# One of four modulation vectors moved: from column blocks visited by TensorE in attention to whole rows summed by VectorE beside w_conv_out

## The chip, the core and the metric

The kernel runs on one core of a Trainium2 chip. A core has five engines that run on their own and meet through semaphores: TensorE (PE, with its weight loads PEld), VectorE (DVE), ScalarE (ACT), GpSimd (POOL) and SyncE (SP), whose queue issues nearly all of this kernel's DMAs, in order. The metric is the device time of one execution in microseconds. Every run computes one trunk layer for 128 context tokens and 512 latent tokens, 640 in all, with 1024 features.

## The reference

All weights are float32. `silu(c)` for the latent tokens and `silu(c_ctx)` for the context tokens each go through `w_ada` (1024 x 6144) and give six vectors of 1024: shift, scale and gate of the mixer, shift, scale and gate of the feed-forward part.

```
ada = silu(c) @ w_ada + b_ada          # one row for latent, one for context tokens
sh1, sc1, g1, sh2, sc2, g2 = split(ada, 6)
u = rms_norm(h, g_pre1) * (1 + sc1) + sh1
z = u @ w_in                           # q, k, v, B, C, x, gate_att, gate_conv
A  = attention(q, k, v) @ w_att_out
Bm = (B * dwconv3(C * x)) @ w_conv_out
h = h + g1 * rms_norm((sigmoid(ga) * A + sigmoid(gc) * Bm) @ w_o, g_post1)
u = rms_norm(h, g_pre2) * (1 + sc2) + sh2
h = h + g2 * rms_norm((silu(g) * val) @ w_down, g_post2)   # [g, val] = dwconv3(u @ w_up)
```

The change is about `g2`, the last sixth of `w_ada`'s columns. It is needed only at the very end, multiplied with `g_post2`, as one row per kind of token that is spread over all partitions.

## The kernel before

Each large product is done as three products of float32r parts: a weight tile is loaded as `raw`, ACT rounds it to `whi`, DVE subtracts to `wlo`, and TensorE does hi x hi, hi x lo and lo x hi (`mm3`, L182). The raw, hi and lo tiles come from rings of three buffers each. The order on TensorE, ACT and DVE is written out by hand: these engines work in program order. SP's order is made by a planner; its queue is strictly in order, and a DMA that waits holds back those behind it. Landings are counted on eight semaphores in turn.

The stages, with the start of each in the profiled execution: a prologue (0 to 62 us) with the first modulation and k, v; attention (62 to 264) for four key groups `g`, nine steps `i` each; w_att_out and a mixer stage of 19 pairs of columns of w_in (`mix`, L1252), to 564; w_conv_out in eight blocks of 128 columns (loop at L1416, 564 to 621); w_o in two halves, the first half in four quarters `q` (L1794); w_up, and w_down woven into it.

The remaining four vectors of the modulation, `g1`, `sc2`, `sh2` and `g2`, are computed in attention. A column block of 128 of w_ada is a DMA of 1024 x 128 elements (`ada_load`, L228), with rows of 512 bytes. `ada_mm` (L231) multiplies it: eight float32 products with 32 columns of `s32` as weights, in which the two vectors silu(c) and silu(c_ctx) stand in columns 30 and 31 of each 32; a slice of `s32` shifted by the row number puts the two results in their rows. The products go round over the four column strips of TensorE. Thirty-two blocks are done at places (g, i) of the steps, one or two at a time: `VISITS` (L682) says where, and a ring of loads (`ring`, L689) brings column blocks and the weight units of att_out through the same raw buffers. After each visit DVE adds the result into `acc` (`ada2_keep`, L252). At the end of attention `ada2_fold` (L260) sums over the strips, adds the bias, multiplies by the gains, and writes `mod`; `mod_rows` (L273) transposes all 64 rows and stores them to `bct` in DRAM, from which `bload` (L1464) later spreads a row over the partitions: `g1` into WR before w_o, `g2` into G2 near the end (L2034).

In the loop of w_conv_out, block j makes the split of block j + 1 (`vcut`, L1248), loads block j + 3 (`mload`, L1224), does two products over 320 tokens (`plain_gemm`, L1200), multiplies each by the gate (`times`), adds the attention branch, has ACT round the result and DVE subtract it (`minus`, L1155). Block 3's column block is loaded twice, at the end of the mixer and in this loop; the second load is the one used. The regions r0 and r1 hold UH and UL, the parts of u, until the last mix; from w_o's last quarter they hold parts of the next stage (ZB0, ZB1), and in between they are free.

Of the kernel before, what the change touches and what calls it, by code (L numbers as in the profile page):

```python
# [11 lines left out]
F32 = mybir.dt.float32  # L12
# [5 lines left out]
D = 1024  # L18
# [45 lines left out]
def trunk_layer(ctx, tc, x_prompt, x_sample, cache_k, cache_v, c, c_ctx, w_ada, b_ada, g_pre1, g_post1, g_pre2,  # L64
# [145 lines left out]
    feat = const.tile([128, 120], F32, name="feat")  # L210
    F_B, F_PRE1, F_POST1, F_PRE2, F_POST2, F_CONV = 16, 64, 72, 80, 88, 96
    scsh = const.tile([128, KT, 4], F32, name="scsh")
    mod = const.tile([128, 4, 2, KT], F32, name="mod")
    bct = dp.tile([64, 128], F32, name="bct")
    hd = dp.tile([NT, 128, D], F32, name="hd")
    actd = dp.tile([NJ, 128, NACT], F32, name="actd")
# [11 lines left out]
    def ada_load(raw, c0):  # L228
        nc.sync.dma_start(raw.rearrange("p (k c) -> p k c", c=128), w_ada[:, c0:c0 + 128].rearrange("(k p) c -> p k c", p=128))
# [10 lines left out]

    def ada2_load(i, room=None):
        ada_raw[i] = raw_tile() if room is None else room
        ada_load(ada_raw[i], (2, 4, 3, 5)[i // KT] * D + (i % KT) * 128)

    def ada2_mm(us, p=None):

# [13 lines left out]
    def ada2_fold(acc):  # L260
        p = ps1()
        for i in range(2):
            PE.matmul(p[:, 32 * i:32 * i + 32], acc[:, i * 128:(i + 1) * 128], sel, start=True, stop=True)
        for which in range(4):
            src = p[:, 16 * which:16 * which + 16].rearrange("p (f r) -> p r f", r=2)
            b = F_B + (2, 4, 3, 5)[which] * KT
            V.tensor_tensor(out=mod[:, which], in0=src, in1=feat[:, b:b + KT].unsqueeze(1).broadcast_to((128, 2, KT)), op=ALU.add)
            if which != 2:
                gn = (F_POST1, F_PRE2, None, F_POST2)[which]
                V.tensor_tensor(out=mod[:, which], in0=mod[:, which], in1=feat[:, gn:gn + KT].unsqueeze(1).broadcast_to((128, 2, KT)),  # L270
                                op=ALU.mult)

    def mod_rows(i0, n, pool, pt):  # L273

        m = n * 2 * KT
        PE.transpose(pt[0:m, 0:128], mod[:, i0:i0 + n].rearrange("p i r f -> p (i r f)"), ident)
        mrow = pool.tile([64, 128], F32, tag="mrow", name=nm("mrow"), bufs=1)
        V.tensor_copy(mrow[0:m, :], pt[0:m, 0:128])
        nc.sync.dma_start(bct[i0 * 2 * KT:i0 * 2 * KT + m, :], mrow[0:m, :])
# [312 lines left out]
    with tc.tile_pool(name="att", bufs=2) as at:  # L592
# [87 lines left out]


        VISITS = {}  # L682
        for at_, n in (((0, 4), 2), ((0, 6), 2), ((0, 8), 2), ((1, 1), 1), ((1, 4), 2), ((1, 6), 1), ((1, 8), 2), ((2, 1), 1), ((2, 4), 2),
                       ((2, 6), 1), ((2, 8), 2), ((3, 1), 2), ((3, 4), 2), ((3, 6), 2), ((3, 8), 2)):
            k = 6 + sum(len(x) for x in VISITS.values())
            VISITS[at_] = tuple(range(k, k + n))
        assert VISITS[3, 8][-1] == 4 * KT - 1
# [638 lines left out]
    for j in range(KT):  # L1326
        unit = next_unit()
        if j == 6:
            for n in range(3):
                mload(n)  # L1330
        if j < 6:
            for f in making[2 * j:2 * j + 2]:
                f()
        elif j == 7:
            adds = msums(0)
            adds[0]()
            mhi(0, 0)
            lo_of(("m", 0, 0))
            adds[1]()
            mhi(0, 1)  # L1340
            adds[2]()
            mload(3)
        outs = plain_gemm(j, *unit.parts, AH, AL)
        for out, (b0, b1) in zip(outs, BLKS):
            if j < 2:
                times(MA[:, j, b0:b1], out, MA[:, KT - 2 + j, b0:b1])
            else:
                S.activation(MA[:, j, b0:b1], out, AF.Copy)
        if j == 0:
            mod_rows(0, 4, sm_, bank(7))  # L1350


    BH = Halves(NTOK, F32R, "BH")
# [11 lines left out]
    def sigma(x, sign=1.0):  # L1365
        S.activation(x, x, AF.Sigmoid, scale=sign)
# [46 lines left out]
    mix_last(NP - 1)  # L1413
    sigma(ROWS[6])
    sigma(ROWS[7], -1.0)
    for j in range(KT):  # L1416
        if j + 1 < KT:
            vcut(j + 1)
        else:
            cut_upto(state["next"] + 1)  # L1420
        if j + 3 < KT:
            mload(2 * NP + j + 3)
        else:
            fetch(state["next"] + min(j - 4, 2))
        _, hi, lo = cut["v", j]
        outs = plain_gemm(j + 2, hi, lo, BH, BL)
        sg = ROWS[j]
        for out, (b0, b1) in zip(outs, BLKS):
            times(sg[:, b0:b1], out, sg[:, b0:b1])
        V.tensor_tensor(out=sg, in0=sg, in1=MA[:, j, :], op=ALU.add)  # L1430
        mh, ml = MH[j // 4][:, j % 4, :], ML[j // 4][:, j % 4, :]
        S.activation(mh, sg, AF.Copy)
        minus(ml, sg, mh.bitcast(F32))
# [9 lines left out]
    ZB0 = ra.tile([128, 4, 4, HALF], F32R, tag="r0", name="ZB0")  # L1443
    ZB1 = ra.tile([128, 4, 4, HALF], F32R, tag="r1", name="ZB1")
    ZB2, ZB3 = (ra.tile([128, 2, 4, HALF], F32R, tag=f"r2{x}", name=f"ZB{i}") for x, i in (("a", 2), ("b", 3)))
    for i, (z, a) in {"B11": (ZB0, 0), "B21": (ZB0, 2), "B22": (ZB1, 0), "T2": (ZB1, 2), "T1": (ZB2, 0), "T3": (ZB3, 0)}.items():
        TT[i] = (z[:, a], z[:, a + 1])
# [6 lines left out]
    def lent(name):  # L1454

        return tuple(x.rearrange("p k c -> p (k c)")[:, :1024] for x in TT[name])
# [337 lines left out]
    for q in range(4):  # L1794
        us.append(next_unit())
        if q == 0:
            half_load(3)
            taps_load()
            for t in range(3):
                row_load(t)  # L1800
            half_cut(3, lent("T3"))
        elif q == 1:
            half_load(0)
            half_cut(0)
        elif q == 2:
            half_load(1)
            plain_load(0, 0)
            plain_load(0, 1)
            ffn_taps(bank(7))
        else:  # L1810
            half_cut(1)
            half_load(2)
            for i, name in ((0, "T2"), (1, "T1")):
                hi_of((0, i), raws[0, i], lent(name))
                lo_of((0, i))
                plain_load(1, i)
        for t in range(NT):
# [315 lines left out]
```

## Time and profile before

| what | value |
|---|---|
| runs | 1118.63, 1118.83, 1120.03 us; median 1118.83 |
| the profiled execution | 1118.44 us, span 1116.3 us |
| TensorE's granted clock | 0.999 |
| moved by DMA | 129.60 MB, mean 116 GB/s |
| w_ada loads in attention | 512 KB each, median 4.0 us to landing |

The span is the time from the first to the last instruction of the program; 2.1 us of the execution lie around it. In the profile's rows a matmul's length includes the depth of its pipeline, so that of two neighbours the distance from start to start is the cost, not the length. "Idle before" is the time that an engine sat still before an instruction, with what released it.

### The profile page before, as it was taken

Reading aid. Unit: us, or ns where it says so; the run is one execution under the profiler, and the core shown is the slowest. Engines: PE = TensorE matmul, PEld = TensorE weight load, DVE = VectorE, ACT = ScalarE, POOL = GpSimd, SP = SyncE. Lnnn points to the kernel's source line nnn. Section 1 sums busy time; section 2 is a strip of 40 time slices with the busy share of each in tenths; the row PEclk is TensorE's granted clock in tenths of the full one; section 3 lists DMA queues with packets and bytes.
Section 4 is the critical chain, followed back from the end, with each engine's and each line's share of the span. In section 5 each row is a group of like instructions: output and inputs, shape, how many; then the busy total and the mean of one; then the engine's idle time right before and its main releaser. Section 6 shows DMA issues by size and latency. Waiting matters only on the chain.

```text
span 1116.3 us, 19771 instructions
## 1 busy us (share of the span) xinstructions
PE 1106.7 (99%) x7963; PEld 1021.7 (92%) x7963; DVE 795.9 (71%) x1305; ACT 577.3 (52%) x1020; POOL 146.8 (13%) x189
## 2 busy tenths in 40 slices
PE   8999999999999999999999999999999999999997
PEld 6788888888999999999999889999999999998886
DVE  5687766654647798889645457888888888889544
ACT  5576666665234454545522256654655455556432
POOL 1066566552000000000000012000000000000001
PEclk9999999999999999999999999999999999999999
DMA  9844223323222233223332644232333233315722
GB/s 325 240 126 141 85 72 105 104 77 115 77 77 76 77 95 95 76 78 97 92 113 74 212 151 155 72 112 90 117 107 101 91 108 107 118 62 179 261 95 95
DMA packets 177305, 129.60 MB, mean 116 GB/s; under 512 B 6274, under 2 KB 159422, under 8 KB 177214
## 3 DMA queue, kind: packets, MB, share of 16 engines
q1 hardware_dynamic: 177102, 128.30, 37.3%
q8 instruction: 63, 1.03, 0.4%
q14 instruction: 28, 0.23, 0.1%
q10 hardware_dynamic: 112, 0.04, 0.0%
HBM read 116.87 MB, written 11.45 MB: 115 GB/s over the span
## 4 chain that ended last, share of the span: by engine, by line
PE 97%; DMA 1%; DVE 1%; ACT 0%; SPq 0%; POOL 0%; issue 0%; DVEq 0%; ACTq 0%; POOLq 0%
PE b L1142 45%; PE b L185 9%; PE b L183 9%; PE b L184 9%; PE s L862 3%; PE s L183 3%; PE s L672 3%; PE s L886 3%; PE s L184 3%; PE s L185 3%; PE s L235 1%; PE s L383 1%; PE b L1679 1%; DMA araw<-in_w_ada_dram 1%; PE s L643 0%; PE b L1530 0%
## 5 line engine op out<-in xcount | busy, mean ns | idle before, releaser
L1142 PE MATMUL b<-ZB,whi 128*128 128x320 f32 x1024 | 226.1, 309 | 0.0
L1142 PEld LDWEIGHTS b<-ZB,whi 128*128 128x128 f32 x1024 | 171.9, 188 | 1.8
L1142 PE MATMUL b<-ZB,wlo 128*128 128x320 f32 x512 | 158.1, 309 | 0.0
L1142 PE MATMUL b<-MT,whi 128*128 128x320 f32 x608 | 134.3, 309 | 0.0
L1142 PEld LDWEIGHTS b<-MT,whi 128*128 128x128 f32 x608 | 101.6, 188 | 0.0
L1142 PEld LDWEIGHTS b<-ZB,wlo 128*128 128x128 f32 x512 | 96.2, 188 | 0.0
L1142 PE MATMUL b<-MT,wlo 128*128 128x320 f32 x304 | 94.1, 309 | 0.0
L849 POOL TENSOR_TENSOR pr<-pr,sm 128x640 f32<-128x640 f32 x64 | 80.0, 1260 | 58.2 <-DVE sm L848 55.8
L1129 ACT ACTIVATE whi<-SUM 128x1024 fp32r<-128x1024 f32 x40 | 42.2, 1055 | 77.3 <-DVE SUM L1594 74.8
L1624 DVE SCALAR_TENSOR_TENSOR Y<-C,cffn,Y 128x642 f32<-128x642 f32 x88 | 77.8, 884 | 0.9
L839 ACT ACTIVATE pr<-s,mx,rq 128x640 f32<-128x640 f32 x64 | 56.6, 885 | 34.7 <-DVE mx L826 31.2
L149 DVE TENSOR_TENSOR wlo<-raw,whi 128x1024 fp32r<-128x1024 f32 (+1 forms) x32 | 35.4, 1107 | 51.7 <-ACT whi L148 48.1
L1142 PE MATMUL b<-UL,whi 128*128 128x320 f32 x228 | 70.9, 311 | 0.0
L1142 PE MATMUL b<-UH,wlo 128*128 128x320 f32 x228 | 70.1, 307 | 0.0
L1142 PE MATMUL b<-UH,whi 128*128 128x320 f32 x228 | 69.4, 304 | 0.0
L1129 ACT ACTIVATE whi<-WB 128x1024 fp32r<-128x1024 f32 x38 | 40.1, 1055 | 55.7 <-DVE WB L1237 55.7
L1133 DVE TENSOR_TENSOR wlo<-raw,whi 128x1024 fp32r<-128x1024 f32 (+1 forms) x51 | 50.5, 1020 | 25.1 <-ACT whi L1129 24.3
L183 PE MATMUL s<-whi,UH 128*128 128x256 f32 (+1 forms) x197 | 64.0, 325 | 0.0
L821 DVE TENSOR_REDUCE mx<-s 128x1 f32<-128x640 f32 x64 | 52.5, 820 | 15.5 <-PE s L672 15.0
L1150 ACT ACTIVATE p<-b 128x320 f32<-128x320 f32 x78 | 34.1, 437 | 54.0 <-PE b L1142 52.1
L185 PE MATMUL s<-whi,UL 128*128 128x256 f32 (+1 forms) x197 | 59.9, 304 | 0.0
L184 PE MATMUL s<-wlo,UH 128*128 128x256 f32 (+1 forms) x197 | 59.8, 303 | 0.0
(354 smaller groups left out, 2945.7 us busy)
## 6 DMA issues: line engine op xcount, KB each, us to landing
raw<-in_w_in_dram SPq DMA_DIRECT2D x48, 512.0 KB, 3.7
RAW<-in_w_up_dram SPq DMA_DIRECT2D x40, 512.0 KB, 3.9
raw<-in_w_ada_dram SPq DMA_DIRECT2D x30, 512.0 KB, 4.0
raw<-in_w_down_dram SPq DMA_DIRECT2D x22, 512.0 KB, 5.6
actd<-Y SPq DMA_DIRECT2D x18, 321.0 KB, 2.5
XT<-in_w_ada_dram SPq DMA_DIRECT2D x9, 512.0 KB, 7.0
raw<-in_w_conv_out_dram SPq DMA_DIRECT2D x9, 512.0 KB, 3.6
raw<-in_w_att_out_dram SPq DMA_DIRECT2D x8, 512.0 KB, 3.6
```

Source lines behind the costliest of these rows:

```text
L149: V.tensor_tensor(out=lo[:, :n], in0=raw, in1=hi[:, :n].bitcast(F32), op=ALU.subtract)
L183: PE.matmul(out, ah, bh, start=start, stop=False)
L184: PE.matmul(out, ah, bl, start=False, stop=False)
L185: PE.matmul(out, al, bh, start=False, stop=stop)
L821: V.tensor_reduce(out=mx, in_=self.sc[h], axis=AX.X, op=ALU.max, negate=True)
L839: S.activation(pr, self.sc[h], AF.Exp, bias=mx, scale=rs, accum_out=sm)
L849: G.tensor_tensor(out=pr, in0=pr, in1=sm.broadcast_to((128, NTOK)), op=ALU.mult)
L1129: S.activation(to[0], raw, AF.Copy)
L1133: V.tensor_tensor(out=lo, in0=raw, in1=hi.bitcast(F32), op=ALU.subtract)
L1142: PE.matmul(out, p[:, ws], q[:, k, :], start=start and k == 0 and n == 0, stop=stop and k == 3 and n == 2, skip_group_check=True)
L1150: S.activation(t, pair[j][b], AF.Copy)
L1624: V.scalar_tensor_tensor(out=y, in0=crows(j)[i][:, d:d + NACT], scalar=cffn[:, 44 * d + o:44 * d + o + 1], in1=y, op0=ALU.mult, op1=ALU.add)
```

## The change

`mod` keeps three vectors; the eight column blocks of `g2` leave the ring and the visits, so that eight places of attention go from two blocks to one. `g2` is made in another way: eight loads of 128 whole rows of w_ada's last 1024 columns (4 KB a row) go into the free regions r0 and r1. For each load DVE multiplies the 128 x 1024 tile by silu(c), one number per partition, and adds it to a sum, and the same for silu(c_ctx): two operations per load, the first pair without the addition. They stand in blocks 1 to 7 of w_conv_out, one between the two `times` and one before ACT's rounding is used, and the last pair in w_o's first quarter. Four float32 products with `ones` (128 x 32) as weights then sum over the partitions, two halves of the columns times two rows, each on its own column strip; they stand in w_o's third quarter, behind the transposes of the convolution taps. DVE adds the bias, multiplies by sqrt(1024) and g_post2, which four DMAs have spread over 64 partitions each, and four stores of 2 KB put the result where `bload` reads it. The tiles of r0 and r1 for the next stage are declared later (`more_right`).

```
-    mod = const.tile([128, 4, 2, KT], F32, name="mod")
+    mod = const.tile([128, 3, 2, KT], F32, name="mod")
+    ones = const.tile([128, 32], F32, name="ones")
+    G.memset(ones, 1.0)
...
-        ada_load(ada_raw[i], (2, 4, 3, 5)[i // KT] * D + (i % KT) * 128)
+        ada_load(ada_raw[i], (2, 4, 3)[i // KT] * D + (i % KT) * 128)
...
-        for which in range(4):
+        for which in range(3):
...
-        for at_, n in (((0, 4), 2), ((0, 6), 2), ((0, 8), 2), ((1, 1), 1), ((1, 4), 2), ((1, 6), 1), ((1, 8), 2), ((2, 1), 1), ((2, 4), 2),
-                       ((2, 6), 1), ((2, 8), 2), ((3, 1), 2), ((3, 4), 2), ((3, 6), 2), ((3, 8), 2)):
+        for at_, n in (((0, 4), 2), ((0, 6), 2), ((0, 8), 2), ((1, 1), 1), ((1, 4), 1), ((1, 6), 1), ((1, 8), 1), ((2, 1), 1), ((2, 4), 1),
+                       ((2, 6), 1), ((2, 8), 1), ((3, 1), 1), ((3, 4), 1), ((3, 6), 1), ((3, 8), 1)):
...
-            mod_rows(0, 4, sm_, bank(7))
+            mod_rows(0, 3, sm_, bank(7))
...
+    GA0, GA1 = (region(ra, f"r{i}", [5, D], F32, f"GA{i}") for i in range(2))
+    gacc, gvec = GA0[:, 0:2, :], GA0[:, 4, :].rearrange("p (i c) -> p i c", i=2)
+    graws = [GA1[:, k, :] for k in range(5)] + [GA0[:, k, :] for k in (2, 3)] + [GA1[:, 0, :]]
+
+    def g2_load(k):
+        nc.sync.dma_start(graws[k], w_ada[k * 128:(k + 1) * 128, 5 * D:6 * D])
+
+    def g2_vectors():
+
+        for i, src in enumerate((b_ada[5 * D:6 * D].unsqueeze(0), g_post2)):
+            for h in range(2):
+                nc.sync.dma_start(gvec[64 * h:64 * h + 64, i, :], src[:, h * 512:h * 512 + 512].broadcast_to((64, 512)))
+
+    def g2_add(k, row):
+        x = s32[:, 32 * k + 30 + row:32 * k + 31 + row]
+        if k == 0:
+            V.tensor_scalar(out=gacc[:, row, :], in0=graws[k], scalar1=x, scalar2=None, op0=ALU.mult)
+        else:
+            V.scalar_tensor_tensor(out=gacc[:, row, :], in0=graws[k], scalar=x, in1=gacc[:, row, :], op0=ALU.mult, op1=ALU.add)
+
+    def g2_rows(p):
+
+        for h in range(2):
+            for row in range(2):
+                j = 64 * h + 32 * row
+                PE.matmul(p[j:j + 32, :], ones, gacc[:, row, h * 512:h * 512 + 512], start=True, stop=True, tile_position=(0, j),
+                          skip_group_check=True)
+        out = GA0[:, 3, 0:512]
+        V.tensor_tensor(out=out, in0=p, in1=gvec[:, 0, :], op=ALU.add)
+        V.scalar_tensor_tensor(out=out, in0=out, scalar=D ** 0.5, in1=gvec[:, 1, :], op0=ALU.mult, op1=ALU.mult)
+        for h in range(2):
+            for row in range(2):
+                j, r0 = 64 * h + 32 * row, (6 + row) * KT + 4 * h
+                nc.sync.dma_start(bct[r0:r0 + 4, :].rearrange("(o f) c -> o (f c)", o=1), out[j:j + 1, :])
+
     for j in range(KT):
+        if j == 0:
+            g2_load(0)
+        if j < KT - 1:
+            g2_load(j + 1)
+        if j == 5:
+            g2_vectors()
...
-        for out, (b0, b1) in zip(outs, BLKS):
+        for h, (out, (b0, b1)) in enumerate(zip(outs, BLKS)):
             times(sg[:, b0:b1], out, sg[:, b0:b1])
+            if h == 0 and j:
+                g2_add(j - 1, 0)
         V.tensor_tensor(out=sg, in0=sg, in1=MA[:, j, :], op=ALU.add)
+        if j:
+            g2_add(j - 1, 1)
...
@@ first quarter of w_o (q == 0), behind half_cut(3, lent("T3"))
+            for row in range(2):
+                g2_add(KT - 1, row)
@@ third quarter of w_o (q == 2), behind ffn_taps(bank(7))
+            g2_rows(bank(6))
@@ fourth quarter of w_o
+            more_right()
```

More of the change, by code (lines that the diff above doesn't have):

```diff
@@ L263, in ada2_fold @@
             PE.matmul(p[:, 32 * i:32 * i + 32], acc[:, i * 128:(i + 1) * 128], sel, start=True, stop=True)
-        for which in range(4):
+        for which in range(3):
             src = p[:, 16 * which:16 * which + 16].rearrange("p (f r) -> p r f", r=2)
-            b = F_B + (2, 4, 3, 5)[which] * KT
+            b = F_B + (2, 4, 3)[which] * KT
             V.tensor_tensor(out=mod[:, which], in0=src, in1=feat[:, b:b + KT].unsqueeze(1).broadcast_to((128, 2, KT)), op=ALU.add)
             if which != 2:
-                gn = (F_POST1, F_PRE2, None, F_POST2)[which]
+                gn = (F_POST1, F_PRE2)[which]
                 V.tensor_tensor(out=mod[:, which], in0=mod[:, which], in1=feat[:, gn:gn + KT].unsqueeze(1).broadcast_to((128, 2, KT)),
@@ L682, in trunk_layer @@
         VISITS = {}
-        for at_, n in (((0, 4), 2), ((0, 6), 2), ((0, 8), 2), ((1, 1), 1), ((1, 4), 2), ((1, 6), 1), ((1, 8), 2), ((2, 1), 1), ((2, 4), 2),
-                       ((2, 6), 1), ((2, 8), 2), ((3, 1), 2), ((3, 4), 2), ((3, 6), 2), ((3, 8), 2)):
+        for at_, n in (((0, 4), 2), ((0, 6), 2), ((0, 8), 2), ((1, 1), 1), ((1, 4), 1), ((1, 6), 1), ((1, 8), 1), ((2, 1), 1), ((2, 4), 1),
+                       ((2, 6), 1), ((2, 8), 1), ((3, 1), 1), ((3, 4), 1), ((3, 6), 1), ((3, 8), 1)):
             k = 6 + sum(len(x) for x in VISITS.values())
             VISITS[at_] = tuple(range(k, k + n))
-        assert VISITS[3, 8][-1] == 4 * KT - 1
+        assert VISITS[3, 8][-1] == 3 * KT - 1
         CUTS = {(0, 1): 10, (0, 3): 11, (0, 8): 12, (1, 2): 13, (1, 8): 14, (2, 2): 15, (2, 8): 16, (3, 6): 17}
@@ L1441, in trunk_layer, with more_right @@
     rows3 = r7[1][:, 4 * NTOK:4 * NTOK + 256].rearrange("p (i c) -> p i c", i=2)
[L1443 to L1447, printed above, removed]
+    for i, x in (("T1", "a"), ("T3", "b")):
+        z = ra.tile([128, 2, 4, HALF], F32R, tag=f"r2{x}", name=f"ZB{i}")
+        TT[i] = (z[:, 0], z[:, 1])
+    def more_right():
+        for names, tag in ((("B11", "B21"), "r0"), (("B22", "T2"), "r1")):
+            z = ra.tile([128, 4, 4, HALF], F32R, tag=tag, name=f"ZB{tag}")
+            for a, i in enumerate(names):
+                TT[i] = (z[:, 2 * a], z[:, 2 * a + 1])
     QUAD = {f"{i + 1}{j + 1}": UFS[i][:, :, j * HALF:(j + 1) * HALF] for i in range(2) for j in range(2)}
```

## The prediction

> **What bounds the kernel now.** I read the page's busy times, slices and chain first, then the windows of the stages that the diff touches, then single instructions there.
>
> ```profile
> span 1116.3 us, 19771 instructions
> ...
> PE 1106.7 (99%) x7963; PEld 1021.7 (92%) x7963; DVE 795.9 (71%) x1305; ACT 577.3 (52%) x1020; POOL 146.8 (13%) x189
> ...
> PE 97%; DMA 1%; DVE 1%; ACT 0%; SPq 0%; POOL 0%; issue 0%; DVEq 0%; ACTq 0%; POOLq 0%
> ```
>
> The chain of waits is TensorE for 97% of the span, so time comes from TensorE instructions removed or added, and from waits newly put in front of TensorE. The windows of four stages (prologue, attention, w_conv_out, first half of w_o) have these columns: length, busy time and count of PE, PEld, DVE, ACT and POOL, granted clock, DMA share, GB/s.
>
> ```profile
> 0.00:62.00 62.00, 58.51 (x459) 45.68 (x460) 39.03 (x101) 33.73 (x66) 8.29 (x24) 1.00 0.93 286
> 62.00:264.00 202.00, 201.69 (x2180) 169.48 (x2179) 139.79 (x375) 136.56 (x303) 122.95 (x130) 1.00 0.33 96
> 564.00:621.00 57.00, 57.00 (x390) 56.96 (x389) 28.10 (x38) 14.46 (x18) 0.00 (x0) 1.00 0.33 97
> 622.60:633.20 10.60, 10.60 (x48) 8.78 (x47) 4.32 (x4) 3.29 (x4) 0.00 (x0) 1.00 1.02 371
> ```
>
> In attention TensorE sits idle for 0.3 of 202 us, and in w_conv_out never. There DVE is busy for only half of the time (28.1 of 57) and the DMA engines for a third: the room in which the moved work must fit.
>
> **The change part by part. Visits removed.** Of the 15 places in attention where TensorE does part of w_ada, eight that did two column blocks now do one: (1,4), (1,8), (2,4), (2,8), (3,1), (3,4), (3,6), (3,8). The timeline shows a single and a double visit, each with the instruction after it (start, length, engine, line):
>
> ```profile
> 127.16 0.64 PE L235 MATMUL s<-raw,s 128*32 128x128 f32 x16
> 127.74 0.42 PE L672 MATMUL s<-KH,QH 64*128 64x320 f32 x2
> ...
> 143.60 1.08 PE L235 MATMUL s<-raw,s 128*32 128x128 f32 x32
> 144.61 0.42 PE L672 MATMUL s<-KH,QH 64*128 64x320 f32 x2
> ```
>
> From start to next start a single visit takes 0.58 us and a double one 1.01, so the second visit costs 0.43 and some 0.15 is paid once per place. Eight times 0.43 is 3.44 us off TensorE. The places stay 15, and so do the sums that DVE keeps after them; eight 512 KB loads leave SP's queue, in a stage where DMA is busy a third of the time. Whether the 3.44 arrives at the end depends on the other engines, for a step must not become theirs. Here are the windows of a step with a double visit, (1,8), and of one that already has a single visit, (1,6):
>
> ```profile
> 160.86:166.50 5.64, 5.64 (x75) 4.12 (x74) 4.62 (x13) 4.41 (x9) 3.06 (x4) 1.00 0.00 0
> 150.23:155.43 5.20, 5.20 (x59) 3.69 (x58) 4.18 (x12) 3.67 (x8) 2.54 (x4) 1.00 0.02 3
> ```
>
> The step with a single visit runs its 5.20 us with TensorE always busy, beside 4.18 us of DVE. Step (1,8) shrunk to 5.21 holds 4.62 of DVE and 4.41 of ACT, which still fits, and the step after it has no visit. I take the whole 3.44; the bounds are 3.44 and, if these chains held every step, nothing.
>
> The fold of the sums loses two DVE operations on 128x16 and the transpose goes from 64 to 48 rows; DVE waits there, not TensorE, and both count as nothing. The memset of `ones` on POOL stands in the prologue, where POOL has 8.29 us of work in 62; nothing.
>
> **Work added on DVE.** In blocks j = 1 to 7 of w_conv_out DVE gets two whole-row operations, 128x1024, before the block's last product and before its `minus`; two more follow in w_o's first quarter. One block's DVE work now, and the two forms of the same shape elsewhere (mean ns after the bar):
>
> ```profile
> 578.60 0.49 DVE L1321 TENSOR_TENSOR WA<-b,WA 128x320 f32<-128x320 f32 x1 [2.31 <-PE b L185]
> 579.12 0.82 DVE L1430 TENSOR_TENSOR WA<-WA,MA 128x640 f32<-128x640 f32 x1
> 580.75 0.82 DVE L1156 TENSOR_TENSOR MLa<-WA,MHa 128x640 fp32r<-128x640 f32 x1 [0.81 <-ACT MHa L1432]
> 581.70 1.23 DVE L1133 TENSOR_TENSOR wlo<-raw,whi 128x1024 fp32r<-128x1024 f32 x1
> 582.84 0.48 DVE L1321 TENSOR_TENSOR WA<-b,WA 128x320 f32<-128x320 f32 x1
> 585.65 0.49 DVE L1321 TENSOR_TENSOR WA<-b,WA 128x320 f32<-128x320 f32 x1 [2.32 <-PE b L185]
> ...
> L1513 DVE SCALAR_TENSOR_TENSOR WR<-TX,root,WR 128x1024 f32<-128x1024 f32 x5 | 6.4, 1285 | 0.9 <-POOL root L1505 0.7
> L1521 DVE TENSOR_SCALAR TX<-WR,root 128x1024 f32<-128x1024 f32 x5 | 3.8, 752 | 4.0 <-POOL root L1505 4.0
> ```
>
> A block takes 585.65 - 578.60 = 7.05 us, of which DVE is busy 3.84. Two operations at 1.285 (0.752 in the first pair) make 6.41, still below 7.05. One fills the 0.81 that DVE spends waiting for ACT's rounding, the other part of the 2.32 before the block's end. The split that TensorE needs, `wlo` of the block after next, ends at 582.93 now; with `minus` 0.48 us later (1.285 less the 0.81) it ends near 583.4, two microseconds before block 3 starts at about 585.4 (DVE takes up block 2's last product at 585.65). Cost nothing; cover gone, each microsecond of DVE over 7.05 costs one per block.
>
> In w_o the same happens once more:
>
> ```profile
> 624.02 1.23 DVE L149 TENSOR_TENSOR wlo<-raw,whi 128x1024 fp32r<-128x1024 f32 x1
> ...
> 626.30 1.22 DVE L149 TENSOR_TENSOR wlo<-raw,whi 128x1024 fp32r<-128x1024 f32 x1
> 634.39 1.23 DVE L1133 TENSOR_TENSOR wlo<-raw,whi 128x1024 fp32r<-128x1024 f32 x1 [6.86 <-ACT whi L1129]
> ...
> 620.71 0.39 PE L183 MATMUL b<-whi,MHa 128*128 128x512 f32 x1
> ...
> 634.34 0.43 PE L1481 MATMUL b<-ident,UFb 88*128 88x88 f32 x2
> ```
>
> TensorE's first two quarters of w_o run from 620.71 to 634.34, 6.8 us each. The second quarter's split would end at 625.25 + 0.48 = 625.7, before 627.5. The last pair of sums (2.57) delays the third quarter's split from 627.5 to 630.6, before 634.34, and falls into DVE's 6.86 us of idleness. The two operations of `g2_rows` behind it, on half that width (an estimated 0.7 us each, somewhat over half of the 1.23 and 1.285), follow the third quarter's tap copies and stand ahead of splits for w_o's second half alone. Nothing; if the 6.86 us of cover were gone, the third quarter would start up to 2.6 late.
>
> **Loads added, on SP's queue.** Eight row loads of 512 KB and four broadcasts of 128 KB join it; four small stores to `bct` wait in it for `g2_rows`, with w_o's last load and w_up's behind them, whose raw buffers DVE frees only later. In the changed program SP issues: conv_out block 2; two w_ada loads, which wait for TensorE's last read of UL in the last mix; an unused conv_out load; five more w_ada loads; three broadcasts; only then the load that block 3 uses. A DMA also waits until the one eight before it has landed, so the broadcasts wait for the first w_ada loads and block 3's load for the third.
>
> ```profile
> raw<-in_w_conv_out_dram SPq DMA_DIRECT2D x9, 512.0 KB, 3.6
> ...
> 562.16 6.62 SPq L1222 DMA_DIRECT2D raw<-in_w_conv_out_dram  x4
> ...
> 562.24 0.31 PE L1142 MATMUL b<-UL,whi 128*128 128x320 f32 x1
> ...
> 580.62 1.04 ACT L1129 ACTIVATE whi<-raw 128x1024 fp32r<-128x1024 f32 x1
> ```
>
> Block 3's load, issued within the 6.62 us before, would stand behind nine loads of 524 KB and three of 131 KB: 5.64 MB with its own. At 371 GB/s (the window of full DMA share) one load moves in 1.4 of its 3.6 us, so data starts 2.2 us after issue: 562.16 + 2.2 + 15.2 = 579.6. That is before ACT's rounding of it at 580.62, and costs nothing. At the prologue's 286 GB/s it is 562.16 + 2.2 + 19.7 = 584.1, then 1.04 and 1.23 of splitting, 586.4: 1.0 us late. I take the first value, whose window has the same queue and the same kinds of loads.
>
> **Work added on TensorE.** Four products of `ones` with 128x512 stand between the tap transposes and w_o's third quarter. A visit has 16 instructions, four rounds over four 32-column strips at 128 columns, in 0.43 us: 0.107 a round. The four products are 8 instructions, two rounds of 512 columns: 2 x 4 x 0.107 = 0.86, and the 0.15 of a place, 1.01 us. All of it lies on the path. If the strips did not run at once it would be 4 x 0.86 + 0.15 = 3.6; the nearest row is the visit's, so 1.0.
> The Trainium skill (TensorE: Matmul & The Clock Gate, Part 3: Packing small matmuls) gives three column tiles at 512 columns a speedup of 2.38 rather than 3, by which the two rounds would be an estimated 1.08 and the sum 1116.6; no row of this trace has 512 columns on strips.
>
> **The sum.** 3.44 - 1.01 = 2.43 us off. The profiled execution took 1118.44 us (span 1116.3 and 2.1 around it), which gives 1116.0; the median of the runs, 1118.83, lies 0.39 above that execution, so **1116.4**.
>
> **The rivals.** Block 3 waits for its load: the queue stands in order, and nine loads go ahead of one that now has an empty queue; against it speaks the 371 GB/s. At 286 GB/s the price is 1.0 and the time 1117.4; from 264 GB/s down the wait eats the whole gain, and below 240 the change is slower by over 0.2%, 1121.1.
> Attention's steps stay as long as they are, because the chain of maximum, exponent, share and transpose sets them and not TensorE: the time would be 1118.83 + 1.01 = 1119.8. Against it speaks the 5.20 step; if only the two steps with a weight split, (1,8) and (2,8), kept their length, 0.86 is lost and it is 1117.3.
> The strips run one after another: 1118.83 - 3.44 + 3.6 = 1119.0. The visits' 0.43 us speaks against it, though at a quarter of the width.
> DVE becomes the bound in w_conv_out: this needs over 1.6 us for one summing operation. At 1.95 each block is 0.69 over, seven blocks 4.8, and the time 1121.2. The five operations of the same form at 1.285 speak against it.
>
> **How the numbers follow.** About 0.2% (2.2 us, below 1116.6 or above 1121.1) is what a measurement of this kernel can tell from no change, and my forecast lies just outside. The forecast as it stands, with small waits or none, gets 0.72, of which 0.47 is past that bound and 0.25 short of it; the late load 0.12 (0.09 within, 0.03 slower), attention's chain 0.06 (0.05 and 0.01), serial strips 0.05 (0.04 and 0.01), DVE 0.05 (0.01 and 0.04). That makes faster 0.47, same 0.44, slower 0.09. Low end: the ones without the 0.15 of a place, 1116.2, and 0.7 for scatter between runs, 1115.5. High end: the partial cases of the late load and attention's chain up to 1119.0; beyond lie about 0.12.
>
> **What would show it.** In the profile after: steps (1,4) to (3,8) 0.43 shorter, with single visits of 0.58; `ones` products of 1.0 us at the third quarter; two operations of 1.29 on DVE in each 7.05 us block, with TensorE never idle; ACT's rounding for block 3 not released by a DMA; span near 1113.9. Wrong if a block of w_conv_out is longer than 7.05, if TensorE idles in attention, or if the ones take over 1.3.

## The result, and the profile after

The changed kernel takes 1116.05 us (median of 9 runs, 1115.57 to 1116.58) against 1118.74 for the kernel before, timed beside it (9 runs, 1118.12 to 1120.03): a ratio of 0.9977, 95% interval 0.9968 to 0.9986, so 2.7 us or some 0.2% faster (1.6 to 3.6 us by the interval). The forecast was 1116.4. The profiled execution took 1116.05 us with a span of 1114.3.

The page's span, busy times and chain after:

```profile
span 1114.3 us, 19557 instructions
...
PE 1104.1 (99%) x7843; PEld 1018.2 (91%) x7843; DVE 813.0 (73%) x1321; ACT 577.3 (52%) x1020; POOL 146.8 (13%) x190
...
PE 95%; DMA 3%; DVE 1%; ACT 1%; POOL 0%; issue 0%; DVEq 0%; SPq 0%; ACTq 0%
```

TensorE has 120 instructions fewer (8 x 16 of the removed visits against 8 of `ones`) and 2.6 us less busy time. DVE has 17 us more and hides them: TensorE is as full as before. The 3% of DMA in the chain, 32 us, lies in the first 35 us, ahead of attention. Windows of the changed kernel: attention from the first step's scores to the last step's, step (1,8), and 57 us of w_conv_out (length, busy time and count of PE, PEld, DVE, ACT, POOL, granted clock, DMA share, GB/s):

```profile
71.17:255.62 184.45, 184.12 (x1897) 153.85 (x1896) 129.21 (x347) 125.18 (x272) 111.49 (x115) 1.00 0.26 76
161.01:166.21 5.20, 5.20 (x59) 3.68 (x58) 4.18 (x12) 3.97 (x8) 2.62 (x4) 1.00 0.00 0
560.00:617.00 57.00, 57.00 (x390) 57.00 (x389) 42.22 (x52) 14.59 (x18) 0.00 (x0) 1.00 0.58 177
```

The same stretch of attention in the kernel before:

```profile
70.60:258.13 187.53, 187.22 (x2009) 156.99 (x2009) 129.82 (x347) 125.16 (x272) 111.23 (x115) 1.00 0.32 94
```

Attention is 187.53 - 184.45 = 3.08 us shorter over seven of the eight places, 0.44 each; the eighth, (3,8), lies in the last step behind the window. Step (1,8) went from 5.64 to 5.20. The two profiled spans differ by 2.0 us only, because the prologue ended 0.57 later in the profile after (71.17 against 70.60, within the scatter of the experiments' profiles): 8 x 0.44 = 3.52, less 0.99 for the `ones` (below), less 0.57, is 1.96. In w_conv_out DVE works 42.2 of 57 us instead of about 28, and TensorE still does not idle.

The timeline of TensorE in the changed kernel at the single visit of (1,8), and at the products of `ones`:

```profile
165.64 0.64 PE L237 MATMUL s<-raw,s 128*32 128x128 f32 x16
166.21 0.33 PE L674 MATMUL s<-KCH,QH 64*128 64x128 f32 x2
...
631.77 1.07 PE L1445 MATMUL b<-GA,ones 128*32 128x512 f32 x8
632.76 0.50 PE L183 MATMUL b<-whi,MHb 128*128 128x512 f32 x1
```

The visit takes 0.57 from start to next start, the `ones` 632.76 - 631.77 = 0.99. And one block of DVE in w_conv_out, from the addition of a block's second product to the next:

```profile
590.29 0.83 DVE L1477 TENSOR_TENSOR WA<-WA,MA 128x640 f32<-128x640 f32 x1
591.03 1.28 DVE L1438 SCALAR_TENSOR_TENSOR GA<-GA,s,GA 128x1024 f32<-128x1024 f32 x1
592.23 0.82 DVE L1158 TENSOR_TENSOR MLa<-WA,MHa 128x640 fp32r<-128x640 f32 x1
592.97 1.22 DVE L1135 TENSOR_TENSOR wlo<-raw,whi 128x1024 fp32r<-128x1024 f32 x1
594.10 0.48 DVE L1323 TENSOR_TENSOR WB<-b,WB 128x320 f32<-128x320 f32 x1
594.50 1.28 DVE L1438 SCALAR_TENSOR_TENSOR GA<-GA,s,GA 128x1024 f32<-128x1024 f32 x1
596.82 0.49 DVE L1323 TENSOR_TENSOR WB<-b,WB 128x320 f32<-128x320 f32 x1 [1.04 <-PE b L185]
597.35 0.83 DVE L1477 TENSOR_TENSOR WB<-WB,MA 128x640 f32<-128x640 f32 x1
```

The block is still 597.35 - 590.29 = 7.06 us. Both sums take 1.28, and DVE then still waits 1.04 for TensorE.

One place looks less comfortable. ACT's rounding of block 3's columns, and SP's issue of their load, in the changed kernel's timeline:

```profile
569.83 0.38 SPq L1224 DMA_DIRECT2D raw<-in_w_conv_out_dram  x1
...
577.04 0.74 ACT L1481 ACTIVATE MHa<-WA 128x640 fp32r<-128x640 f32 x1 [5.37 <-DVE WA L1477]
579.48 1.06 ACT L1131 ACTIVATE whi<-raw 128x1024 fp32r<-128x1024 f32 x1 [1.70 <-DMA raw<-in_w_conv_out_dram]
```

ACT waited 1.70 us for that load. It landed some 9.6 us after its issue.

### The profile page after: what moved, and what is told of

It is laid out like the page before. It is cut to its first block, busy times and chain, and to the rows that moved or that the text cites. A ratio compares the mean times of both kernels' runs of the same rounds, so it can differ in the third digit from the quotient of the medians.

```text
span 1114.3 us, 19557 instructions
## 1 busy us (share of the span) xinstructions
PE 1104.1 (99%) x7843; PEld 1018.2 (91%) x7843; DVE 813.0 (73%) x1321; ACT 577.3 (52%) x1020; POOL 146.8 (13%) x190
## 3 DMA queue, kind: packets, MB, share of 16 engines
q8 instruction: 62, 1.02, 0.4%
## 4 chain that ended last, share of the span: by engine, by line
PE 95%; DMA 3%; DVE 1%; ACT 1%; POOL 0%; issue 0%; DVEq 0%; SPq 0%; ACTq 0%
PE b L1144 45%; PE b L185 9%; PE b L183 9%; PE b L184 9%; PE s L864 3%; PE s L674 3%; PE s L888 3%; PE s L183 3%; PE s L184 3%; PE s L185 3%; DMA araw<-in_w_ada_dram 2%; PE s L237 1%; DMA XT<-in_w_ada_dram 1%; PE b L1733 1%; PE s L645 0%; PE b L1584 0%
## 5 line engine op out<-in xcount | busy, mean ns | idle before, releaser
L1144 PE MATMUL b<-ZBr,whi 128*128 128x320 f32 x688 | 152.1, 309 | 0.0
L1144 PEld LDWEIGHTS b<-ZBr,whi 128*128 128x128 f32 x688 | 115.0, 188 | 0.1
L1144 PE MATMUL b<-ZBr,wlo 128*128 128x320 f32 x344 | 106.2, 309 | 0.0
L1131 ACT ACTIVATE whi<-SUM 128x1024 fp32r<-128x1024 f32 x40 | 42.2, 1055 | 77.3 <-DVE SUM L1648 74.8
L1144 PE MATMUL b<-ZBT,whi 128*128 128x320 f32 x320 | 71.1, 309 | 0.0
L1144 PEld LDWEIGHTS b<-ZBr,wlo 128*128 128x128 f32 x344 | 64.7, 188 | 0.0
```

The lines of the kernel that those rows point to most:

```text
L1131: S.activation(to[0], raw, AF.Copy)
L1144: PE.matmul(out, p[:, ws], q[:, k, :], start=start and k == 0 and n == 0, stop=stop and k == 3 and n == 2, skip_group_check=True)
```

## The experiments

Each kernel was timed beside the kernel before; those medians are 1118.24 (e1 to e4), 1118.40 (e5 to e8) and 1118.44 (e9). The intervals of these ratios are some 0.17 to 0.3% wide, about as much as the effects sought. The profiles are finer: the last column is the time from attention's first product of scores to the start of w_conv_out's last addition (DVE, block 7), less the changed kernel's 618.51 - 71.17 = 547.34. It leaves out the prologue, whose end lies anywhere from 70.45 to 72.19 us in these profiles; in those of e1, e4 and e5 the clock was at 0.50 for a while there (last section).

| kernel | median us | against before, us | ratio, 95% interval | stretch against changed, us |
|---|---|---|---|---|
| changed | 1116.05 | -2.69 | 0.9968 to 0.9986 | 0 |
| e1 visits only | 1114.67 | -3.57 | 0.9953 to 0.9978 | +0.01 |
| e2 no `ones` | 1114.75 | -3.49 | 0.9951 to 0.9978 | +0.22 |
| e3 nine places | 1117.32 | -0.92 | 0.9981 to 0.9999 | +1.72 |
| e4 one load for block 3 | 1115.60 | -2.64 | 0.9969 to 0.9986 | -0.04 |
| e5 six visits fewer | 1115.52 | -2.88 | 0.9962 to 0.9983 | -0.45 |
| e6 three sums | 1117.65 | -0.75 | 0.9982 to 1.0000 | +2.70 |
| e7 `ones` on one strip too | 1119.24 | +0.84 | 0.9998 to 1.0016 | -0.01 |
| e8 block 3 loaded again | 1123.02 | +4.62 | 1.0024 to 1.0055 | +7.79 |
| e9 twelve places | 1116.82 | -1.62 | 0.9976 to 0.9994 | +0.87 |

**e1 and e2: the gain and its price apart.** e1 keeps the single visits and nothing else:

```diff
-    ones = const.tile([128, 32], F32, name="ones")
-    G.memset(ones, 1.0)
...
-        if j == 0:
-            g2_load(0)
-        if j < KT - 1:
-            g2_load(j + 1)
-        if j == 5:
-            g2_vectors()
...
-            if h == 0 and j:
-                g2_add(j - 1, 0)
...
-            g2_rows(bank(6))
...
-        bload(G2[:, row, :], 3, row)
+        bload(G2[:, row, :], 0, row)
```

> Only the single visits stay; all the work on the second gate is left out (no ones, no row loads, no sums on DVE, no four products; the gate's rows are read from the first gate's place instead, so the second residual is scaled by a wrong gate). My theory (a second visit costs TensorE 0.43 us and everything else added but the four products is hidden): 8 x 0.43 = 3.44 us below the kernel before, 1115.3 against its 1118.74, and 0.8 to 1.0 below the changed kernel's 1116.05. Rival, attention's other chains hold part of the steps: only 2 to 2.7 below before, 1116 to 1116.7, as fast as the changed kernel, and TensorE idle inside attention. Rival, the sums or the loads cost something that the trace of the changed kernel hides (a longer prologue by the memset, for one): more than 3.44 below.

e2 keeps all but the four products:

```diff
-        for h in range(2):
-            for row in range(2):
-                j = 64 * h + 32 * row
-                PE.matmul(p[j:j + 32, :], ones, gacc[:, row, h * 512:h * 512 + 512], start=True, stop=True, tile_position=(0, j),
-                          skip_group_check=True)
         out = GA0[:, 3, 0:512]
-        V.tensor_tensor(out=out, in0=p, in1=gvec[:, 0, :], op=ALU.add)
+        V.tensor_tensor(out=out, in0=gacc[:, 0, 0:512], in1=gvec[:, 0, :], op=ALU.add)
```

> The changed kernel without the four products of ones: DVE takes the gate's rows from one partition's partial sums instead, so the second gate is wrong; loads, sums, vectors and stores stay. My theory: 1.0 us below the changed kernel, 1115.05, equal to the kernel with the single visits alone within 0.3. Rival, the sums and loads cost something although TensorE shows no idle time: slower than the single visits alone by over 0.5. Rival, the tap copies and splits behind the products set the third quarter's start, not the products: less than 0.5 below the changed kernel.

Measured: -3.57 and -3.49 against before, where 3.44 was forecast for the visits. The two agree to 0.1, so sixteen sums, eight loads, four broadcasts and the memset cost the medians nothing that they can tell, which is little, as the interval of each is over 2.5 us wide. The stretch tells more: it holds thirteen of the sixteen sums, all loads and all broadcasts and ends ahead of the `ones`, and it is the same within 0.01 with them (changed kernel) and without (e1). From e2 to the changed kernel it is 0.80, where the trace has 0.99 for the `ones`. In e2's stretch there is 0.22 that e1 does not have; e5 shows what such a piece is.

**e3 and e9: the visits in fewer places.** If a place cost 0.15 by itself, pairs at fewer places would be cheaper. e3 puts the 18 visits at nine:

```diff
-        for at_, n in (((0, 4), 2), ((0, 6), 2), ((0, 8), 2), ((1, 1), 1), ((1, 4), 1), ((1, 6), 1), ((1, 8), 1), ((2, 1), 1), ((2, 4), 1),
-                       ((2, 6), 1), ((2, 8), 1), ((3, 1), 1), ((3, 4), 1), ((3, 6), 1), ((3, 8), 1)):
+        for at_, n in (((0, 4), 2), ((0, 6), 2), ((0, 8), 2), ((1, 4), 2), ((1, 8), 2), ((2, 4), 2), ((2, 8), 2), ((3, 4), 2), ((3, 8), 2)):
```

> The changed kernel with the same 18 visits in attention put as nine pairs, at the nine places (0,4), (0,6), (0,8), (1,4), (1,8), (2,4), (2,8), (3,4), (3,8), instead of three pairs and twelve singles at 15 places. My theory (0.43 per visit and 0.15 once per place): six places fewer, 6 x 0.15 = 0.9 us below the changed kernel, 1115.15. Rival, the 0.15 belongs to a visit and not to its place (a fill that each visit pays, overlapped by chance in the pairs): no change, 1116.05. Rival, the pairs make steps whose weight arrives late from a ring of three buffers, or steps that DVE sets: TensorE idle there, 1116.1 or more.

It was 1.77 us slower than the changed kernel, each against before, not 0.9 faster, and the 1.72 of its stretch agrees. The windows of step (1,6), now without a visit, and of the step behind it, and the timeline where they meet, in e3:

```profile
150.27:154.90 4.63, 4.63 (x44) 3.31 (x43) 3.61 (x10) 3.27 (x7) 2.26 (x3) 1.00 0.00 0
154.90:160.75 5.85, 5.82 (x49) 5.23 (x48) 3.33 (x11) 3.59 (x7) 4.72 (x6) 1.00 0.01 3
```

```profile
154.46 0.82 DVE L868 COPY PT<-s 128x640 f32<-128x640 f32 x1 [0.63 <-PE s L863]
154.90 0.18 PEld L674 LDWEIGHTS s<-KH,QH 64*128 64x128 f32 x1 [0.17 <-ACT AHa L892]
155.34 0.18 PEld L674 LDWEIGHTS s<-KH,QH 64*128 64x128 f32 x1 [0.26 <-DVE PT L868]
```

Step (1,6) lost its 0.57 (5.21 in the changed kernel, 4.63 here). But the next step's second product of scores comes 0.44 after the first instead of 0.25 or less: it starts at 155.34, just when DVE's copy of the turned probabilities ends (154.46 + 0.82 = 155.28). The two meet in PSUM, the memory that TensorE writes its results to. From the first product of scores to the first product behind them it is 156.41 - 154.90 = 1.51 here and 156.66 - 155.58 = 1.08 in the changed kernel, which is the whole of the difference between the two steps (5.85 here, 5.43 there): there the visit stands in that time, and the next step finds its banks free. The busy time of 5.82 in 5.85 hides this, for the time between two products of one group is counted as busy.

e5 tests this by itself: six single visits are left out and nothing is put elsewhere.

```diff
-        for at_, n in (((0, 4), 2), ((0, 6), 2), ((0, 8), 2), ((1, 1), 1), ((1, 4), 1), ((1, 6), 1), ((1, 8), 1), ((2, 1), 1), ((2, 4), 1),
-                       ((2, 6), 1), ((2, 8), 1), ((3, 1), 1), ((3, 4), 1), ((3, 6), 1), ((3, 8), 1)):
+        for at_, n in (((0, 4), 2), ((0, 6), 2), ((0, 8), 2), ((1, 4), 1), ((1, 8), 1), ((2, 4), 1), ((2, 8), 1), ((3, 4), 1), ((3, 8), 1)):
...
```

> The changed kernel with the single visits at (1,1), (1,6), (2,1), (2,6), (3,1) and (3,6) left out altogether (six column blocks of the modulation are missing, so it is wrong); nothing is put elsewhere. The kernel with nine pairs showed that a step without its single visit runs 0.57 us shorter, but that the next step's first product of scores then waits 0.36 to 0.65 us, mostly for DVE's copy of the turned probabilities out of PSUM. New theory: a place's first visit fills that wait and costs net 0.14, so six fewer give 6 x 0.14 = 0.85 us below the changed kernel: 2.69 + 0.85 = 3.5 below before. Rival, the prediction's price (0.58 for a single visit, all of it on the path): 3.4 below the changed kernel, 6.1 below before. Rival, the pairs of that kernel were late with their weights and the places had no part in it: anything up to 3.4.

The window of the same stretch of attention in e5, and the weight loads of the scores that wait behind steps (1,1) and (1,6):

```profile
71.64:255.12 183.48, 182.90 (x1802) 152.56 (x1801) 127.89 (x341) 125.23 (x272) 111.35 (x115) 1.00 0.20 59
...
128.60 0.18 PEld L674 LDWEIGHTS s<-KH,QH 64*128 64x128 f32 x1 [0.19 <-ACT pr L840]
155.70 0.18 PEld L674 LDWEIGHTS s<-KH,QH 64*128 64x128 f32 x1 [0.26 <-DVE PT L868]
```

184.45 - 183.48 = 0.97 us for six visits, 0.16 each. The rival of the prediction's price (3.4) is out. Each of the six steps lost 0.57, and the step behind each grew by 0.36 to 0.44. Behind the (r,6), r from 1 to 3, the scores wait for DVE's copy as in e3; behind the (r,1) they wait for ACT's exponent (`pr`), which also reads its input from PSUM. So a lone visit costs 0.57 where it stands and saves 0.4 behind it, and a second visit at the same place costs its full 0.43. That gives e3 as well: 6 x (0.43 - 0.16) = 1.6, against 1.72 measured.

Of the median, -2.88, only 0.2 of the 0.85 expected is seen. 0.5 of the rest is in w_conv_out, below.

e9 asks whether the places (1,4), (2,4) and (3,4) are such places too (with block 3's single load of e4):

```diff
-        for at_, n in (((0, 4), 2), ((0, 6), 2), ((0, 8), 2), ((1, 1), 1), ((1, 4), 1), ((1, 6), 1), ((1, 8), 1), ((2, 1), 1), ((2, 4), 1),
-                       ((2, 6), 1), ((2, 8), 1), ((3, 1), 1), ((3, 4), 1), ((3, 6), 1), ((3, 8), 1)):
+        for at_, n in (((0, 4), 2), ((0, 6), 2), ((0, 8), 2), ((1, 1), 1), ((1, 6), 1), ((1, 8), 2), ((2, 1), 1),
+                       ((2, 6), 1), ((2, 8), 2), ((3, 1), 1), ((3, 6), 1), ((3, 8), 2)):
```

> The changed kernel with block 3's columns loaded once (as in the run on the unused load) and with the single visits at (1,4), (2,4) and (3,4) moved to (1,8), (2,8) and (3,8), which become pairs: 12 places for the 18 visits. What moves is three times 0.43 us for a second visit, against what a place's only visit is worth to TensorE there. Theory of the run with six fewer (a lone visit fills a wait for PSUM at every such place and is worth 0.16 net): attention 3 x (0.43 - 0.16) = 0.8 us longer, 0.8 above the kernel with one load. Rival, only the places ahead of (r,2) and (r,7) have that wait and (r,4) has none: 3 x 0.15 = 0.45 us shorter attention, which the trace shows to 0.05 and the medians hardly. In both, no wait of ACT for block 3's load, and w_conv_out at 7.05 a block.

They are: 1.02 slower than e4 by the medians against before, 0.91 by the stretch, 0.8 expected. The windows of step (1,4) without its visit and of the step behind it, in e9:

```profile
140.19:144.82 4.63, 4.63 (x44) 3.30 (x43) 3.15 (x8) 3.16 (x7) 4.11 (x5) 1.00 0.35 105
144.82:150.85 6.03, 6.00 (x51) 5.41 (x50) 3.57 (x12) 3.97 (x8) 4.70 (x6) 1.00 0.01 3
```

5.20 became 4.63, and the next step's 5.61 became 6.03; there too the scores wait 0.26 for DVE's copy. Of the three arrangements of the 18 visits that were tried, that of the changed kernel is the best.

**e4, e5 and e8: block 3's load.** Block 3's columns of w_conv_out are loaded twice in both kernels; the first load is never read. e4 uses the first, which stands ahead of five row loads:

```diff
         elif n < 2 * NP + KT:
-            col_load(("v", n - 2 * NP), w_conv_out, (n - 2 * NP) * 128)
+            if n != 2 * NP + 3 or ("v", 3) not in raws:
+                col_load(("v", n - 2 * NP), w_conv_out, (n - 2 * NP) * 128)
```

> The changed kernel with block 3's columns of w_conv_out loaded once: the first of its two loads, which nothing read, is now the one that is used, and it stands ahead of five row loads and three broadcasts instead of behind them. My theory: ACT's rounding for block 3 no longer waits for a DMA (it stood idle 1.70 us for it), and the time stays at 1116.05 within 0.4, because that wait ended 0.7 us before TensorE would have missed the split. Rival, the late load costs time somewhere that the window of w_conv_out does not show (a later buffer, a later load): 0.5 us or more below the changed kernel.

ACT's rows for block 3 in e4:

```profile
578.03 0.74 ACT L1482 ACTIVATE MHa<-WA 128x640 fp32r<-128x640 f32 x1 [5.36 <-DVE WA L1478]
578.67 1.04 ACT L1131 ACTIVATE whi<-raw 128x1024 fp32r<-128x1024 f32 x1
```

The wait is gone and the time is the same (-2.64 against -2.69), as expected. But the wait is not the same in every profile. ACT's rounding and TensorE's first products of block 3 in e5, whose loads there are those of the changed kernel:

```profile
580.34 1.06 ACT L1130 ACTIVATE whi<-raw 128x1024 fp32r<-128x1024 f32 x1 [3.10 <-DMA raw<-in_w_conv_out_dram]
```

```profile
582.12 0.31 PE L184 MATMUL b<-BL,whi 128*128 128x320 f32 x1
582.71 0.42 PE L185 MATMUL b<-BHa,wlo 128*128 128x320 f32 x1 [0.29 <-DVE wlo L1134]
```

There ACT waits 3.10 instead of 1.70, and TensorE waits for `wlo`: 0.59 between two products that are 0.15 apart otherwise, 0.44 lost, and 0.1 more behind it. That is the 0.5 by which e5's stretch (-0.45) is behind its attention (-0.97); e2's 0.22 has the same look, with ACT waiting 2.80 there.

e8 loads block 3's columns a second time into the same buffer:

```diff
         if j + 3 < KT:
             mload(2 * NP + j + 3)
+            if j == 0:
+                nc.sync.dma_start(raws["v", 3].rearrange("p (k c) -> p k c", c=128),
+                                  w_conv_out[:, 3 * 128:4 * 128].rearrange("(k p) c -> p k c", p=128))
```

> The changed kernel with a second copy of block 3's columns of w_conv_out into the same buffer, behind the first, so that ACT's rounding of them can start only when the second has landed. In the changed kernel's profile the load landed at 579.4 and block 3's product started at 582.5, 0.7 us after the split was done. My theory: the copy waits for the first to land and takes 2 to 3.6 us more, so the split comes 1.3 to 2.9 us after TensorE wants it and the kernel is that much slower than the changed one, with one wait of TensorE ahead of block 3 and none before it. Rival, TensorE has more in hand than the 0.7 us, or gets the time back later: within 0.4 of the changed kernel.

It was 7.3 us slower than the changed kernel, not 1.3 to 2.9. ACT and TensorE in e8, and the windows of the wait (whole, its first half and its end), of the 4.6 us behind it and of the next 3.9:

```profile
586.43 1.06 ACT L1131 ACTIVATE whi<-raw 128x1024 fp32r<-128x1024 f32 x1 [8.84 <-DMA raw<-in_w_conv_out_dram]
```

```profile
587.54 0.63 PE L183 MATMUL b<-BHa,whi 128*128 128x320 f32 x1 [5.07 <-ACT whi L1131]
587.97 0.47 PE L184 MATMUL b<-BL,whi 128*128 128x320 f32 x1
588.80 0.63 PE L185 MATMUL b<-BHa,wlo 128*128 128x320 f32 x1 [0.36 <-DVE wlo L1135]
```

```profile
582.47:587.54 5.07, 0.00 (x1) 0.01 (x1) 0.02 (x1) 1.06 (x1) 0.00 (x0) 0.78 0.69 207
582.47:585.00 2.53, 0.00 (x0) 0.00 (x0) 0.00 (x0) 0.00 (x0) 0.00 (x0) 1.00 1.01 271
585.50:587.54 2.04, 0.00 (x1) 0.01 (x1) 0.02 (x1) 1.06 (x1) 0.00 (x0) 0.50 0.22 85
587.54:592.14 4.60, 4.24 (x15) 3.84 (x15) 4.57 (x6) 0.51 (x1) 0.00 (x0) 0.51 0.39 112
592.14:596.00 3.86, 3.86 (x28) 3.86 (x28) 3.86 (x5) 1.18 (x2) 0.00 (x0) 1.00 0.06 17
```

The copy landed at 586.4, and TensorE waited 5.07 us. Then came what neither theory had: the granted clock was 0.51 for 4.6 us. It had fallen within the wait, between 585.0 and 585.5, and came back at 592.1, 6.8 us later. Fourteen products took the 4.60 us behind the wait instead of 14 x 0.147 = 2.06. Of these 2.54 some 0.56 is a second wait, for `wlo`: 588.80 - 587.97 = 0.83, where slow products are 0.27 apart. About 2.0 is left for the slow clock. First wait and slow stretch are 5.22 + 2.54 = 7.76, the whole of the stretch's 7.79. The wait itself was longer than expected because the copy came late: its issue stood behind the load of block 5 and waited 2.5 us for the first load to land, until 580.97, and the copy then took 5.5 us to land, where 2 to 3.6 had been expected.

**e6: a third sum.** The edit:

```diff
         if j:
             g2_add(j - 1, 1)
+            V.scalar_tensor_tensor(out=gacc[:, 1, :], in0=graws[j - 1], scalar=s32[:, 32 * j - 2:32 * j - 1], in1=gacc[:, 1, :], op0=ALU.mult, op1=ALU.add)
```

> The changed kernel with a third whole-row operation in blocks 1 to 7 of w_conv_out (the second row's term is added twice, so that row of the gate is wrong). By the prediction's working DVE then has 3.84 + 3 x 1.28 = 7.7 us for a block of 7.05, 0.65 over, in six blocks (in block 1 it has 6.6). My theory: 3.9 us at most, less the lead that DVE has before it (0.7 to 2.0 us), so 1.9 to 3.9 us above the changed kernel, near the kernel before or past it, with TensorE idle in the later blocks of w_conv_out for `whi`/`wlo` or for a bank. Rival, operations of DVE come in time wherever they stand, because three buffers of the split absorb it: within 0.4 of the changed kernel.

1.94 slower than the changed kernel, at the low end. DVE in e6:

```profile
589.41 0.48 DVE L1323 TENSOR_TENSOR WA<-b,WA 128x320 f32<-128x320 f32 x1
...
592.26 1.28 DVE L1438 SCALAR_TENSOR_TENSOR GA<-GA,s,GA 128x1024 f32<-128x1024 f32 x1
593.58 1.28 DVE L1480 SCALAR_TENSOR_TENSOR GA<-GA,s,GA 128x1024 f32<-128x1024 f32 x1
594.78 0.82 DVE L1158 TENSOR_TENSOR MLa<-WA,MHa 128x640 fp32r<-128x640 f32 x1
...
596.65 0.48 DVE L1323 TENSOR_TENSOR WB<-b,WB 128x320 f32<-128x320 f32 x1
```

DVE never waits any more and sets the block: 596.65 - 589.41 = 7.24, 0.19 over 7.05. The durations add up to 7.7, but one operation starts before the end of the one ahead of it: the 1.28 of 593.58 is followed at 594.78, 1.20 later. From start to start of TensorE's products, 0.36 is lost at block 3's split, whose load is late as in e5, 0.19 in each of four later blocks, and 0.7 in the first two quarters of w_o, whose splits DVE brings later: 1.8 in all. The 2.70 of the stretch ends in an instruction of DVE, which lags here.

**e7: strips.** Four more products ahead of the four, all on the first strip:

```diff
     def g2_rows(p):
 
+        for h in range(2):
+            for row in range(2):
+                PE.matmul(p[0:32, :], ones, gacc[:, row, h * 512:h * 512 + 512], start=True, stop=True, tile_position=(0, 0),
+                          skip_group_check=True)
         for h in range(2):
```

> The changed kernel with four more products of ones with 128x512 ahead of the four, all four on the first strip of 32 columns; the result is overwritten by the products that follow. The four on four strips took 0.995 us. My theory, strips are what makes two rounds of eight: the four on one strip run one after the other, two rounds each, 4 x 2 x 0.43 = 3.5 us above the changed kernel, hence 0.8 above before. Rival, a strip of 32 columns costs a quarter by itself, or products on the same strip overlap: 0.9 to 1.0 us above the changed kernel.

3.53 slower than the changed kernel, 3.5 expected. TensorE in e7:

```profile
631.44 3.19 PE L1444 MATMUL b<-GA,ones 128*32 128x512 f32 x7
634.05 0.63 PE L1449 MATMUL b<-GA,ones 128*32 128x512 f32 x3
...
635.85 0.50 PE L183 MATMUL b<-whi,MHb 128*128 128x512 f32 x1
```

All eight products take 635.85 - 631.44 = 4.41, so the four on one strip take 4.41 - 0.99 = 3.4, if the other four cost what they cost alone, against 0.99 on four strips.

## Why the prediction was right

The forecast is 0.35 us above the time measured, and the mechanism was the one named: 3.44 off by the visits, 1.01 on by the `ones`, all else hidden. Of the 0.35, 0.09 is the median of the kernel before, 1118.83 there and 1118.74 here. The medians' interval, 1.6 to 3.6 us, would hold other sums than 2.43 too; what bears it out are the terms in the trace, 3.5 and 0.99. Step by step:

- **Visits: right.** "Eight times 0.43 is 3.44": 3.08 over seven places in the trace, 3.57 in e1. The steps went from 5.64 to 5.20.
- **"Some 0.15 is paid once per place": right as a number, wrong as a reason.** A lone visit takes 0.57 and a second one 0.43, but a place is not a surcharge that the kernel pays: of the 0.57 about 0.4 would be waited anyway, for DVE or ACT to have read a bank of PSUM. For the visits the sum did not need this step, because the change kept all places; the `ones` took their 0.15 from it, and there it came out. A schedule built on it is slower (e3, e9). There was luck in this: the change took out second visits only, and for lone ones the same working would have failed, as six of them bring 0.97 (e5) and not 3.4.
- **Rival "attention's chain": against the change it fails, in other steps it holds.** None of the seven steps in the window kept its length (each lost 0.43 to 0.45). Yet where a lone visit was taken out, the step behind gave back 0.36 to 0.44 of 0.57.
- **DVE: right, and with more room than was worked out.** 6.41 was the forecast of its block; it waits 1.04 of 7.05, so it takes 6.0. The step "each microsecond of DVE over 7.05 costs one" adds up durations, and e6 shows that they overlap: three sums take 7.24 and not 7.7.
- **`ones`: right.** 0.99 against 1.01; e7 has 3.4 / 0.99 = 3.4 times for four strips. The Trainium skill (TensorE: Matmul & The Clock Gate, Part 3: Packing small matmuls) has 2.38 for three; the estimate from it, 1.08 for the rounds and 1.23 with the 0.15, was high for four.
- **Block 3's load: the term that was mis-sized.** "At 371 GB/s ... lands at 579.6", which is 576.7 on the new clock (w_conv_out runs 2.9 earlier). It landed 2.8 later, and "ACT's rounding for block 3 not released by a DMA" was wrong. Windows of the changed kernel from 561.4, where that working has the data start, to the landing:

```profile
569.00:573.00 4.00, 4.00 (x30) 4.00 (x29) 3.04 (x5) 1.69 (x2) 0.00 (x0) 1.00 1.03 411
573.00:576.00 3.00, 3.00 (x22) 3.00 (x22) 1.34 (x3) 0.00 (x0) 0.00 (x0) 1.00 1.07 252
576.00:579.50 3.50, 3.50 (x26) 3.50 (x25) 2.47 (x4) 0.76 (x2) 0.00 (x0) 1.00 1.16 244
...
561.40:579.50 18.10, 18.10 (x125) 18.10 (x124) 8.87 (x12) 5.09 (x8) 0.00 (x0) 1.00 1.07 329
```

The DMA engines are full all through, but they move 411 GB/s until 573 and some 250 at the end. The queue there turns from rows of w_ada to broadcasts and to columns of w_conv_out (128 floats a piece, as `col_load` cuts them); that the pieces' size is the cause was not tried. The prediction's 5.64 MB took 18.1 us, 312 GB/s, between the two rates that it weighed; in the trace data starts at about 560.5 already, which makes it 19.0 us and 297 GB/s. The lateness cost the changed kernel's profiled run nothing, since `wlo` ended at 581.8 and was wanted at 582.8. So the step held by one microsecond, and e2 and e5 lost 0.2 to 0.5 there; what executions without a profile lost is not known. The 0.12 given to this rival was fair, but its price holds for short waits only: the long one of e8 cost the clock as well.

## What to carry to other kernels

Work is worth what it leaves behind when it goes, not its own duration: the second of two visits gave all of its 0.43 us, a lone one only 0.16 of 0.57, because it stood where TensorE would have waited for a bank of PSUM. Look at what the next instruction waits for before removing or merging fillers on the engine that bounds the kernel. A burst of loads put in front of a load that used to have an empty queue should be priced at a rate measured for the same mix of loads: the 371 GB/s of another stage put the landing 2.8 us too early. A duplicate load in that queue can be dropped: with it gone (e4) ACT's wait was gone, though the time stayed.

## What the runs showed of the hardware that was not expected

- After TensorE had idled 5.07 us (e8), the granted clock was 0.51 for 4.6 us and then 1.00 again; with the second wait of 0.56 a wait of 5.2 cost 7.8. The clock fell some 2.8 us into the wait and was down for 6.8 us in all. After the wait of 0.29 in e5 products were 0.15 apart again within two instructions. Shorter waits than e8's can do it too: in the prologue TensorE waits for DVE's `xn`, in e1, e4 and e5 for 1.72 to 1.78 us (with shorter waits of 0.3 to 0.5 near it), and behind each the clock was 0.50 for 3.4 us; with 1.55 (e8's prologue) and 1.21 (e7's) it stayed at 1.00. The Trainium skill (TensorE: Matmul & The Clock Gate, Part 1: The HAM clock gate) has the clock halve after an idle window of about 3.4 us and come back after a busy one of that length. The times at half clock agree, one such length in the prologues and two in e8; the idle time does not, as 1.72 us were enough here. The wait in e4's prologue and a window behind it:

```profile
11.24 3.50 PE L367 MATMUL s<-ident,xn 128*128 128x128 f32 x16 [1.78 <-DVE xn L360]
...
12.00:13.00 1.00, 1.00 (x6) 0.87 (x6) 0.96 (x5) 0.60 (x3) 0.71 (x2) 0.50 1.10 324
```

- The same full DMA engines moved 411 GB/s from 569 to 573 us and 244 from 576 to 579.5 (changed kernel).
- DVE's operations on 128x1024 and 128x640 in a row start up to 0.09 us before the end of the one ahead by the profile (1.28 long, 1.19 to 1.20 from start to start).
